# Value projection of two attention mixers: weight channels standing and tokens streaming, with transposes, instead of tokens standing

## The chip, the cores and the metric

The kernel runs on one core of a Trainium2 chip. Its time is the device time of one execution in microseconds (us). The engines named below are TensorE (PE, with its weight loads PEld), VectorE (DVE), ScalarE (ACT), GpSimd (POOL) and SyncE (SP), which here only issues DMA.

## The reference

One decoder layer over 2048 tokens of width 1024, in float32. An input projection feeds three mixers whose outputs are joined; then come an output projection, a layer norm, a gated feed-forward part with a short convolution, and a second layer norm.

```python
def _token_mixer(h, w_in, conv_w, a_log, dt_bias, gdn_norm_w, lam_vecs, diff_norm_w, w_out, lam_init):
    proj = h @ w_in
    a_qkv, a_z, a_b, a_dec, b_qkv, c_qkv = jnp.split(proj, np.cumsum(IN_SPLITS)[:-1], axis=-1)
    y_a = _gated_deltanet(a_qkv, a_z, a_b, a_dec, conv_w, a_log, dt_bias, gdn_norm_w)
    y_b = _dilated_window_group(b_qkv)
    y_c = _diff_attention_group(c_qkv, lam_vecs, diff_norm_w, lam_init)
    return jnp.concatenate([y_a, y_b, y_c], axis=-1) @ w_out
```

`b_qkv` (768 channels) belongs to the dilated window attention, `c_qkv` (768) to the differential attention. Of each, 256 channels are the values; these 512 value channels are what the change is about. The attention multiplies softmax weights by values, and for this the values are wanted with tokens in the rows (partitions).

## The kernel before, in words

*Blocks of tokens.* The tokens are worked in four blocks of 512 (`TB`). For each block t there is a job "A" (the projections of the two softmax mixers, `Projection.project`), a job "G" (those of the gated delta net), "d" and "w" (differential and dilated attention), and "f" (feed-forward). The lists `FIRST`, `SECOND` and `THIRD` (L1374 to L1376) give the order in which the jobs are written: A0 G0 A1 G1 d0 w0 first; then the steps of the delta net ("i" and "b" the inverse, "p" preparation, "r" recurrence) with G2, G3 and A3 among them; then w1 d1 A2 and the rest with the feed-forward part. A planner (the `TileContext`, L1451) orders the instructions of each engine by its own simulated times, so instructions of d0, which is written after G1, stand between those of A0. Each engine, and each queue of DMA issues, then works strictly in that order.

*Products in three parts.* Each product is made of float32 numbers split into a rounded high part and a low part, as three matmuls: high by high, high by low, low by high. `Dense.weights` (L127) brings a weight of 512 KB in two halves of 256 KB: it loads a raw half (L151), rounds it to the high part on ScalarE (L153) and subtracts on GpSimd for the low part (L154). Raw halves have six buffers, high and low halves four each in A0, A1 and A3. From the job "c0" on (`dn.keep`), the first use of a weight also writes both parts to DRAM (L161), and each later use loads them from there instead (`whi<-whi_d` and `wlo<-wlo_d`, L148), with no cast or subtraction. A0 and A1 come before c0, A3 is the first after it, and A2 comes later.

*Queries and keys.* `Dense.product` (L198) makes one 128 channel x 512 token product: the weight is the standing operand, the tokens stream, 8 x 3 matmuls of 128x512 into one PSUM bank. Before it starts it calls `flush(1)`, which counts down the steps that were put off with `put(n, step)` and writes out those that are due. `Projection.split` (L627) takes the result out of PSUM.

*Values.* `Projection.values` (L642) does it the other way: 128 tokens are the standing operand and 512 value channels stream, so that the result has tokens in its rows. It takes two groups of two token tiles; each group holds two PSUM banks for its whole length and goes through all eight k steps, so each of the four value weights (`w_val`, two k steps each) is brought twice per block, and each use serves 2 x 2 x 3 = 12 matmuls. Each bank is copied out on ScalarE (L662) into `vo`, and SP issues two writes (L663, L664): to `wv_d` (dilated) and `fv_d` (differential). `vo` shares the two buffers of the tag "y" with the results of the queries and keys.

*PSUM.* The tag "d" has two banks for A0 and A1, three for A3, four for A2.

Of the kernel before, what the change touches and what calls it, by code (L numbers as in the profile page):

```python
# [7 lines left out]
F32 = mybir.dt.float32  # L8
# [5 lines left out]
P = 128  # L14
T = 2048
D = 1024
KD = D // P
NB = 4
TB = T // NB
# [71 lines left out]
SLOT = 0.65  # L91
# [19 lines left out]
class Dense:  # L111
# [15 lines left out]
    def weights(self, src, k=KD, m=P, pool=None, key=None):  # L127
# [6 lines left out]
        def put(dt, name):  # L134
# [4 lines left out]
            else:  # L139
                w = self.wp.tile([P, TB], dt, tag=name, name=name, bufs=NRAW if name == "wraw" else NHALF)  # L140
            return shape(w[:, 0:n])

        his, los = [], []
        for i in range(2):
# [4 lines left out]
            else:  # L149
                raw = shape((self.wp.tile([P, TB], F32, tag="w" if self.ring else "wraw", name="wraw", bufs=self.ring or NRAW))[:, 0:n])  # L150
                nc.sync.dma_start(out=raw, in_=src[:, i * (k // 2) : (i + 1) * (k // 2)])  # L151
# [469 lines left out]
class Projection:  # L621
# [20 lines left out]
    def values(self, x, wide, near):  # L642


        nc, dn = self.nc, self.dn
        for g in range(2):
            ps = [dn.ps.tile([P, TB], F32, tag="d", name="vp") for _ in range(2)]
            for j in range(KD // 2):
                whi, wlo = dn.weights(self.I["w_val"][j], k=2, m=TB, key=("val", j))
                for a in range(2):  # L650
                    k = 2 * j + a
                    for i in range(2):
                        sl = slice((2 * g + i) * P, (2 * g + i + 1) * P)
                        xhi, xlo = (v[k][:, sl] for v in x)
                        nc.tensor.matmul(out=ps[i], lhsT=xhi, rhs=whi[:, a], start=(k == 0), stop=False)
                        nc.tensor.matmul(out=ps[i], lhsT=xhi, rhs=wlo[:, a], start=False, stop=False)
                        nc.tensor.matmul(out=ps[i], lhsT=xlo, rhs=whi[:, a], start=False, stop=(k == KD - 1))
                        yield SLOT
            for i in range(2):
                n = 2 * g + i  # L660
                vo = self.ap.tile([P, 2, 2, 2, P], F32, tag="y", name="vo", bufs=NY)[:, 0]
                nc.scalar.copy(vo, ps[i].rearrange("p (a b c) -> p a b c", a=2, b=2))  # L662
                nc.sync.dma_start(out=wide[n * P : (n + 1) * P], in_=vo[:, 0])  # L663
                nc.sync.dma_start(out=near[:, :, n], in_=vo[:, 1])  # L664

    def project(self, t, blocks, pool=None):
        nc, tc, I, dn, ap = self.nc, self.tc, self.I, self.dn, self.ap
# [370 lines left out]
class Ffn:  # L1038
# [131 lines left out]
    def turn(self, r, x):  # L1170
        nc, dn = self.nc, self.dn
        for k in range(KD):
            tp = dn.ps.tile([P, 4, P], F32, tag="d", name="tp")
            for tt in range(4):
                nc.tensor.transpose(tp[:, tt], r[tt][:, k * P : (k + 1) * P], self.ident)
            hi, lo = dn.split(tp.rearrange("p a b -> p (a b)"))
            x[0].append(hi)
            x[1].append(lo)
            yield 0.5
# [92 lines left out]
def decoder(tc, I, out, y_d=None, upto=3):  # L1272
    nc = tc.nc
    with ExitStack() as ctx:
# [52 lines left out]
        gates.close()  # L1327
        dn.wp, dn.ring = ctx.enter_context(tc.tile_pool(name="wp2", bufs=1)), NW
        psd2 = ctx.enter_context(tc.tile_pool(name="psd2", bufs=2, space=PSUM))
# [25 lines left out]
LAG_NT = 2  # L1355
NKS = 4
NW = 14
NRAW = 6
NHALF = 4
NXR = 4  # L1360
NPD = 6
NP = 4
NY = 2
# [15 lines left out]
def host_arrays(inputs):  # L1379
# [3 lines left out]
    a = {}  # L1383
    x = f("x")[0]
    a["xT"] = np.ascontiguousarray(x.reshape(NB, TB, KD, P).transpose(0, 2, 3, 1))

    def tiles(w):
        k, c = w.shape
        return np.ascontiguousarray(w.reshape(k // P, P, c // P, P).transpose(2, 1, 0, 3))
# [7 lines left out]
    a["gdn_a_log"] = np.ascontiguousarray(f("gdn_a_log"))  # L1397

    att = w_in[:, 2056:3592]
    a["w_att"] = tiles(np.concatenate([att[:, 0:512], att[:, 768:1280]], 1))  # L1400
    val = np.concatenate([att[:, 512:768], att[:, 1280:1536]], 1)
    a["w_val"] = np.ascontiguousarray(val.reshape(4, 2, P, TB).transpose(0, 2, 1, 3))
    a["diff_norm"] = np.ascontiguousarray(np.tile(f("diff_norm")[0], 2).reshape(P, 1))
    a["diff_lambda"] = np.ascontiguousarray(f("diff_lambda").reshape(1, 128))

# [15 lines left out]
    i = np.arange(P)  # L1421
    d = i[:, None] - i[None, :]
# [32 lines left out]
```

## Time and profile before

| what | us |
|---|---|
| median of 3 runs | 3210.19 |
| lowest and highest | 3209.55, 3212.74 |
| the profiled execution | 3217.71 |
| its span, first to last instruction | 3216.0 |

The profile describes one execution. Starts are in us from the start of the span; "busy" is the sum of durations with overlaps counted once; what stands in brackets behind an instruction is the idle time of its engine just before it and what released it. Matmuls are pipelined, so the distance between two starts is less than the duration shown. PEclk and "clock" are the granted clock of TensorE as a share of full speed. The mean clock over the execution is 0.964.

### The profile page before, as it was taken

How to read it: one execution, taken by the hardware profiler on the slowest of the kernel's cores; microseconds unless marked ns; L12 is line 12 of the kernel's file. 1: busy time of each engine (PE TensorE's matmuls, PEld its weight loads, DVE VectorE, ACT ScalarE, POOL GpSimd, SP SyncE). 2: the span in 40 equal slices, each digit the busy share in tenths (PEclk: the TensorE clock that was granted, in tenths of full speed). 3: DMA queues.
4: the chain of work that ended last, by engine and by line, in shares of the span. 5: the costliest groups of instructions: out<-in, count | busy, mean ns of one | idle time of the engine just before them, and what ended most of it. 6: DMA issues, size and time to landing. Idle time of an engine off the chain costs nothing.

```text
span 3216.0 us, 43559 instructions
## 1 busy us (share of the span) xinstructions
PE 2999.8 (93%) x14476; PEld 2310.5 (72%) x14476; DVE 1883.0 (59%) x3392; ACT 1358.5 (42%) x3188; POOL 751.0 (23%) x741
## 2 busy tenths in 40 slices
PE   7898989998688699999999999999999999999998
PEld 5676867777467577766777667777778764788887
DVE  2572659665436247855688445556777644474446
ACT  3653453644234134755565343223365545222213
POOL 4563555444332015555141000000000000000001
PEclk9998989999789799999999999999999999999999
DMA  7546464547788688777878446567486644666554
GB/s 212 168 140 203 136 202 140 154 148 217 271 247 299 197 275 272 261 244 238 272 250 266 155 157 205 175 212 246 150 264 202 190 150 125 203 233 195 191 187 147
DMA packets 463329, 659.30 MB, mean 205 GB/s; under 512 B 75168, under 2 KB 201632, under 8 KB 462336
## 3 DMA queue, kind: packets, MB, share of 16 engines
q1 hardware_dynamic: 425024, 567.36, 56.3%
q10 hardware_dynamic: 24480, 44.58, 3.8%
q0 software_dynamic: 13600, 44.58, 3.7%
q8 instruction: 115, 1.88, 0.2%
q14 instruction: 110, 0.90, 0.1%
HBM read 500.82 MB, written 155.39 MB: 204 GB/s over the span
## 4 chain that ended last, share of the span: by engine, by line
PE 62%; DMA 7%; DVE 5%; ACT 2%; issue 1%; SPq 1%; POOL 1%; ACTq 0%; DVEq 0%; POOLq 0%
PE d L206 10%; PE d L207 10%; PE d L208 10%; PE rp L1158 6%; PE rp L1159 6%; PE rp L1161 6%; PE bank L818 4%; PE bank L833 2%; PE bank L767 1%; PE bank L997 1%; DMA whi<-whi_d 1%; PE bank L1004 1%; PE bank L958 1%; DMA fq_d<-sy 1%; DVE nm L772 1%
## 5 line engine op out<-in xcount | busy, mean ns | idle before, releaser
L206 PE MATMUL d<-xhi,whi 128*128 128x512 f32 x2144 | 857.5, 400 | 47.4 <-DMA whi<-whi_d 16.1
L208 PE MATMUL d<-xhi,wlo 128*128 128x512 f32 x2144 | 854.0, 398 | 2.1 <-POOL wlo L154 2.1
L207 PE MATMUL d<-xlo,whi 128*128 128x512 f32 x2144 | 853.1, 398 | 1.3 <-DVE xlo L169 1.3
L154 POOL TENSOR_TENSOR wlo<-wraw,whi 128x512 fp32r<-128x512 f32 x370 | 504.8, 1369 | 1112.0 <-ACT whi L153 897.1
L206 PEld LDWEIGHTS d<-xhi,whi 128*128 128x128 f32 x2144 | 409.4, 191 | 153.3 <-DMA whi<-whi_d 17.2
L208 PEld LDWEIGHTS d<-xhi,wlo 128*128 128x128 f32 x2144 | 408.7, 191 | 105.4 <-issue 16.2
L207 PEld LDWEIGHTS d<-xlo,whi 128*128 128x128 f32 x2144 | 409.5, 191 | 100.2 <-issue 15.0
L153 ACT CAST whi<-wraw 128x512 fp32r<-128x512 f32 x370 | 227.9, 619 | 274.2 <-DMA wraw<-in_w_up 67.0
L1159 PE MATMUL rp<-wlo,hhi 128*128 128x512 f32 x704 | 278.2, 396 | 0.1
L1158 PE MATMUL rp<-whi,hhi 128*128 128x512 f32 x704 | 271.3, 399 | 0.7 <-DVE xlo L169 0.4
L843 POOL TENSOR_SCALAR_AFFINE_SELECT pd<-pd 128x128 f32<-128x128 f32 x64 | 27.4, 430 | 1013.2 <-DVE pd L839 993.5
L1161 PE MATMUL rp<-whi,hlo 128*128 128x512 f32 x672 | 263.9, 396 | 0.0
L776 ACT ACTIVATE bank<-bank,nm 128x512 f32<-128x512 f32 (+3 forms) x320 | 191.1, 598 | 107.4 <-DVE nm L772 66.2
L1090 ACT COPY ub<-d 128x512 f32<-128x512 f32 x172 | 100.8, 586 | 267.6 <-PE d L208 265.2
L839 DVE SCALAR_TENSOR_TENSOR pd<-pe,f_nlam,pd 128x512 f32<-128x512 f32 (+3 forms) x160 | 113.5, 715 | 168.1 <-ACT pe L835 142.6
L772 DVE TENSOR_REDUCE nm<-bank 128x1 f32<-128x512 f32 (+3 forms) x288 | 167.3, 596 | 73.2 <-PE bank L767 68.3
L1158 PEld LDWEIGHTS rp<-whi,hhi 128*128 128x128 f32 x704 | 132.4, 189 | 38.4 <-issue 7.1
L365 DVE SCALAR_TENSOR_TENSOR yc<-ub,i_taps,yc 128x512 f32<-128x512 f32 x144 | 156.5, 1087 | 3.3
L1159 PEld LDWEIGHTS rp<-wlo,hhi 128*128 128x128 f32 x704 | 132.9, 189 | 34.1 <-issue 6.3
L1161 PEld LDWEIGHTS rp<-whi,hlo 128*128 128x128 f32 x672 | 126.8, 189 | 30.8 <-issue 4.0
L1168 DVE TENSOR_TENSOR r<-r,rp 128x512 f32<-128x512 f32 x152 | 101.6, 683 | 79.8 <-PE rp L1161 74.0
L818 PE MATMUL bank<-pd,fv 128*64 128x512 f32 (+3 forms) x320 | 144.7, 554 | 1.4 <-POOL pd L843 0.6
(283 smaller groups left out, 4676.1 us busy)
## 6 DMA issues: line engine op xcount, KB each, us to landing
whi<-whi_d SPq DMA_DIRECT2D x486, 256.0 KB
wlo<-wlo_d SPq DMA_DIRECT2D x486, 256.0 KB
whi_d<-whi ACTq DMA_DIRECT2D x170, 256.0 KB
wlo_d<-wlo POOLq DMA_DIRECT2D x170, 256.0 KB, 3.7
wraw<-in_w_gdn SPq DMA_DIRECT2D x128, 256.0 KB
ks<-fk_d SPq DMA_DIRECT2D x160, 196.0 KB
wraw<-in_w_up SPq DMA_DIRECT2D x86, 256.0 KB
wraw<-in_w_down SPq DMA_DIRECT2D x50, 256.0 KB
```

The costliest lines, as they stand in the source:

```text
L153: nc.scalar.copy(hi, raw)
L154: nc.gpsimd.tensor_tensor(out=lo, in0=raw, in1=hi, op=ALU.subtract)
L206: nc.tensor.matmul(out=ps, lhsT=whi[:, k], rhs=xhi[k], start=(k == 0), stop=False)
L207: nc.tensor.matmul(out=ps, lhsT=whi[:, k], rhs=xlo[k], start=False, stop=False)
L208: nc.tensor.matmul(out=ps, lhsT=wlo[:, k], rhs=xhi[k], start=False, stop=(k == KD - 1))
L365: nc.vector.scalar_tensor_tensor(out=yc, in0=ub[:, j : j + TB], scalar=self.taps[:, mt, j : j + 1], in1=yc, op0=ALU.mult, op1=ALU.add)
L772: nc.vector.tensor_reduce(out=o, in_=s[:, 0:nf], axis=mybir.AxisListType.X, op=ALU.min)
L776: nc.scalar.activation(out=s[:, 0:n], in_=s[:, 0:n], func=AF.Exp, scale=-1.0, bias=o, accum_out=den[:, b, m, qt : qt + 1])
L818: nc.tensor.matmul(out=po[64 * hh : 64 * hh + 64, q0:], lhsT=v[:, 64 * hh : 64 * hh + 64], rhs=pd[hh][:, q0:], start=start, stop=stop)
L1158: nc.tensor.matmul(out=ps, lhsT=hi[:, sl], rhs=whi, start=first, stop=False)
L1159: nc.tensor.matmul(out=ps, lhsT=hi[:, sl], rhs=wlo, start=False, stop=last and lo is None)
L1161: nc.tensor.matmul(out=ps, lhsT=lo[:, sl], rhs=whi, start=False, stop=last)
```

## The change

Values are made like queries and keys: four products of 128 value channels by 512 tokens, with the weight standing. Their weights are appended to `w_att` (tiles 8 to 11), so each is brought once per block and serves 24 matmuls. Each product is copied out to `cm` (four buffers, shared with the raw tokens), and a put-off step turns it: four transposes of 128x128 into one bank of the tag "d", one copy to `vo`, one write issued by ScalarE. With `LAG_VALUES` = 1 the step of product c is written out before product c + 2 starts; `dn.flush()` at the end writes out what is left. Products 0 and 1 are the dilated values, 2 and 3 the differential ones.

```diff
-        for g in range(2):
-            ps = [dn.ps.tile([P, TB], F32, tag="d", name="vp") for _ in range(2)]
-            for j in range(KD // 2):
-                whi, wlo = dn.weights(self.I["w_val"][j], k=2, m=TB, key=("val", j))
-                for a in range(2):
-                    k = 2 * j + a
-                    for i in range(2):
-                        sl = slice((2 * g + i) * P, (2 * g + i + 1) * P)
-                        xhi, xlo = (v[k][:, sl] for v in x)
-                        nc.tensor.matmul(out=ps[i], lhsT=xhi, rhs=whi[:, a], start=(k == 0), stop=False)
-                        nc.tensor.matmul(out=ps[i], lhsT=xhi, rhs=wlo[:, a], start=False, stop=False)
-                        nc.tensor.matmul(out=ps[i], lhsT=xlo, rhs=whi[:, a], start=False, stop=(k == KD - 1))
-                        yield SLOT
-            for i in range(2):
-                n = 2 * g + i
-                vo = self.ap.tile([P, 2, 2, 2, P], F32, tag="y", name="vo", bufs=NY)[:, 0]
-                nc.scalar.copy(vo, ps[i].rearrange("p (a b c) -> p a b c", a=2, b=2))
-                nc.sync.dma_start(out=wide[n * P : (n + 1) * P], in_=vo[:, 0])
-                nc.sync.dma_start(out=near[:, :, n], in_=vo[:, 1])
+        for c in range(4):
+            pp = yield from self.product(8 + c, x)
+            cm = dn.xp.tile([P, TB], F32, tag="xraw", name="vc", bufs=NXR)
+            nc.scalar.copy(cm, pp)
+
+            def turn(c=c, cm=cm):
+                tp = dn.ps.tile([P, 4, P], F32, tag="d", name="vt")
+                for n in range(4):
+                    nc.tensor.transpose(tp[:, n], cm[:, n * P : (n + 1) * P], dn.ident)
+                vo = self.ap.tile([P, 2, 4, P], F32, tag="y", name="vo", bufs=NY)[:, 0]
+                nc.scalar.copy(vo, tp)
+                to = wide.rearrange("(n p) i c -> p n i c", p=P)[:, :, c] if c < 2 else near[:, c - 2]
+                nc.scalar.dma_start(out=to, in_=vo)
+
+            dn.put(LAG_VALUES, turn)
+        dn.flush()
...
+LAG_VALUES = 1
...
-    a["w_att"] = tiles(np.concatenate([att[:, 0:512], att[:, 768:1280]], 1))
-    val = np.concatenate([att[:, 512:768], att[:, 1280:1536]], 1)
-    a["w_val"] = np.ascontiguousarray(val.reshape(4, 2, P, TB).transpose(0, 2, 1, 3))
+    a["w_att"] = tiles(np.concatenate([att[:, 0:512], att[:, 768:1280], att[:, 512:768], att[:, 1280:1536]], 1))
```

## Rows read from the trace of the kernel before

**Rows 1.** The page's first two parts: busy time of each engine, and the span in 40 slices of 80 us, in tenths, for TensorE and its granted clock.

```profile
PE 2999.8 (93%) x14476; PEld 2310.5 (72%) x14476; DVE 1883.0 (59%) x3392; ACT 1358.5 (42%) x3188; POOL 751.0 (23%) x741
...
PE   7898989998688699999999999999999999999998
...
PEclk9998989999789799999999999999999999999999
```

**Rows 2.** Busy time by stretch: the stretch and its length, then PE, PEld, DVE, ACT and POOL busy with the number of instructions, then granted clock, DMA share and GB/s. A0, A1, the first and second half of A3, A2.

```profile
63.60:111.20 47.60, 33.70 (x131) 26.22 (x129) 18.89 (x86) 28.48 (x82) 19.08 (x15) 0.86 0.63 202
289.00:329.50 40.50, 35.03 (x174) 26.58 (x174) 11.52 (x32) 18.18 (x37) 19.87 (x16) 0.92 0.63 216
855.80:895.60 39.80, 20.57 (x49) 11.37 (x47) 8.01 (x21) 3.58 (x6) 10.89 (x12) 0.58 0.79 279
905.00:934.50 29.50, 27.23 (x238) 22.55 (x237) 7.62 (x20) 8.44 (x23) 5.30 (x6) 0.86 0.88 256
1141.70:1188.20 46.50, 40.67 (x230) 31.31 (x229) 17.60 (x50) 12.44 (x23) 2.15 (x2) 0.93 0.82 276
```

**Rows 3.** The instructions that write or read the tile `vo`: duration in ns (least, median, most), first and last start.

```profile
L662 ACT COPY vo<-vp x16: 559/587/602, 92.3 to 1188.7; 128x512 f32<-128x512 f32 x16
L663 SPq DMA_DIRECT2D wv_d<-vo x16: 319/382/1099, 93.6 to 1189.5; - x16
L664 SPq DMA_DIRECT2D fv_d<-vo x16: 525/562/1403, 94.7 to 1190.1; - x16
```

**Rows 4.** TensorE in order of time around A0's values: start, duration, instruction, and in brackets the idle time before it and its releaser.

```profile
77.26 0.66 PE L767 MATMUL bank<-ks,qs 96*128 96x384 f32 x1 [4.05 <-DMA ks<-fk_d]
...
91.95 1.52 PE L767 MATMUL bank<-ks,qs 96*128 96x128 f32 x4 [6.39 <-ACT whi L153]
...
97.30 0.63 PE L657 MATMUL vp<-whi,xlo 128*128 128x512 f32 x1
97.73 0.63 PE L655 MATMUL vp<-whi,xhi 128*128 128x512 f32 x1
...
112.09 0.50 PE L334 MATMUL d<-xhi,i_wba 128*128 128x512 f32 x1 [0.87 <-ACT vo L662]
```

**Rows 5.** SP's queue of DMA issues in order of time in the same stretch.

```profile
69.08 0.53 SPq L151 DMA_DIRECT2D wraw<-in_w_val  x1
76.00 0.31 SPq L741 DMA_DIRECT2D qs<-fq_d  x1
...
78.50 2.36 SPq L151 DMA_DIRECT2D wraw<-in_w_val  x2
89.02 0.34 SPq L736 DMA_DIRECT2D ks<-fk_d  x1
89.45 0.33 SPq L151 DMA_DIRECT2D wraw<-in_w_val  x1
...
90.73 1.78 SPq L151 DMA_DIRECT2D wraw<-in_w_val  x4
```

**Rows 6.** A1's values, in order of time: two instructions of TensorE, and one line of SP's queue.

```profile
303.76 0.43 PE L997 MATMUL bank<-pts,vw 128*64 128x128 f32 x2 [1.75 <-ACT pts L1007]
...
313.37 0.79 PE L655 MATMUL vp<-whi,xhi 128*128 128x512 f32 x1 [3.72 <-ACT vo L662]
...
299.44 14.46 SPq L151 DMA_DIRECT2D wraw<-in_w_val  x7
```

**Rows 7.** TensorE's waits over the whole span, grouped by who waited for whom: us in total, times, the longest.

```profile
PE vp L655 <- ACT whi L153: 17.7, 5, 5.5
...
PE vp L655 <- DMA whi<-whi_d: 7.1, 2, 5.6
```

**Rows 8.** ScalarE's waits from 855 to 897 us, in the same form.

```profile
ACT whi L153 <- DMA x_d<-fs: 8.3, 1, 8.3
...
ACT whi L153 <- DMA r<-in_x: 6.4, 1, 6.4
ACT whi L153 <- DMA wraw<-in_w_val: 5.4, 1, 5.4
```

**Rows 9.** From the page's groups of instructions (busy us, mean ns of one, idle time before) and of DMA issues (count, KB each): the subtraction, the cast, the loads from the DRAM copies and the raw loads of value weights.

```profile
L154 POOL TENSOR_TENSOR wlo<-wraw,whi 128x512 fp32r<-128x512 f32 x370 | 504.8, 1369 | 1112.0 <-ACT whi L153 897.1
...
L153 ACT CAST whi<-wraw 128x512 fp32r<-128x512 f32 x370 | 227.9, 619 | 274.2 <-DMA wraw<-in_w_up 67.0
...
whi<-whi_d SPq DMA_DIRECT2D x486, 256.0 KB
...
wraw<-in_w_val SPq DMA_DIRECT2D x40, 256.0 KB
```

**Rows 10.** Transposes of the dilated attention (L1004): their group; then, in order of time, a set of four of them between value matmuls of A1; then the busy times of the stretch from 296 to 301 us, in which 14 of them stand (columns as in rows 2).

```profile
L1004 PE MATMUL bank<-d_ident,p 128*128 128x128 f32 x400 | 67.0, 279 | 1.2 <-DVE p L978 1.2
...
297.82 0.60 PE L1004 MATMUL bank<-d_ident,p 128*128 128x128 f32 x4
298.18 0.48 PE L656 MATMUL vp<-wlo,xhi 128*128 128x512 f32 x1
298.49 0.39 PE L657 MATMUL vp<-whi,xlo 128*128 128x512 f32 x1
298.72 0.39 PE L656 MATMUL vp<-wlo,xhi 128*128 128x512 f32 x1
...
296.00:301.00 5.00, 5.00 (x30) 4.21 (x29) 1.18 (x2) 0.59 (x2) 2.88 (x3) 1.00 0.26 91
```

## Prediction

> **What bounds the kernel now.** I read the page's first two parts first. TensorE is busy 93% of the span, and in the slices it is at 9 from about 1,250 us on; what it loses it loses before, in the same slices in which the granted clock drops [rows 1]. So the end is set by TensorE's stream, and a change counts by what it adds to that stream and by the waits it takes out of the first 1,200 us. DMA, VectorE and ScalarE count only where TensorE waits for them.
>
> Next I cut out the four stretches in which the value matmuls run, with the busy time of each engine [rows 2]. They belong to A0 (63.6 to 111.2 us), A1 (289.0 to 329.5), A3 (855.8 to 934.5, in two halves with 9 us of other work between) and A2 (1141.7 to 1188.2). The same 96 matmuls are worth 96 x 0.23 = 22 us in each: 0.23 us lies between two starts where nothing is late, though the duration shown is 0.39 (298.49 to 298.72) [rows 10]. TensorE is idle for 47.6 - 33.7 = 13.9 us in A0's stretch, 5.5 in A1's, 39.8 - 20.6 = 19.2 and 2.3 in A3's halves, 5.8 in A2's. The mean clocks are 0.86, 0.92, 0.58, 0.86 and 0.93: after a wait a dozen matmuls start 0.43 apart instead of 0.23 (97.30, 97.73) [rows 4], the lower of the clock's two levels, 1.2 instead of 2.4 GHz.
>
> Last, the instructions themselves, to see what each wait is for.
>
> - A0: 6.39 us at 91.95, for the cast of a value weight; 4.05 at 77.26 is for keys of d0 [rows 4]. SP's queue shows why: nothing is issued from 69.6 to 76.0 and from 80.9 to 89.0 us, and then what stands first is a load of d0's queries or keys; the value weights are behind it [rows 5].
> - A1: 1.75 us, and 3.72 until the two PSUM banks of the first half are copied out; seven value loads take 14.46 us to be issued [rows 6].
> - A3: of the waits before value matmuls, five (17.7 us) are for the cast of a value weight, one per half load, which does only 6 matmuls [rows 7]. In that stretch ScalarE waits 5 to 8 us at a time for DMA before a cast [rows 8].
> - A3's second half and A2: 7.1 us in two waits, the longer 5.6 (A2's), for weights read back from their DRAM copies [rows 7].
>
> **The change, part by part.** *Matmuls*: 96 per block before, 4 x 8 x 3 = 96 after, of the same shape. Nothing.
>
> *Weights.* A value weight of 512 KB is used for 12 matmuls before and for 24 after, so there are 4 fetches per block and not 8. The raw loads go from 40 [rows 9] to 24 (A0 and A1 eight fewer each; A3 had read its second half back), and the loads from the copies fall by 16 + 16 (A3: 8 + 8, A2: 8 + 8). That is 48 x 256 KB = 12.6 MB. In A0 and A1 also 16 casts of 0.62 us on ScalarE and 16 subtractions of 1.37 on GpSimd go [rows 9]; neither engine was the bound there. What the waits are worth then:
>
> - A0: seven of the sixteen value loads are issued after 69.6 us [rows 5], so nine were out before the gaps, and eight is now all there is. At most 6.39 and the low clock after (13 matmuls x 0.2 = 2.6) go: 9.0. The keys of d0 and G0's weights are late next, on the same queue, so I take 8; at the least 0.
> - A1: with seven loads from 299.44 on [rows 6], nine of the sixteen were issued before; eight are needed. 1.75 + 3.72 + 2.6 for the low clock = 8.1 can go. The dilated block that shares the stretch is late next; I take 7, at the least 0.
> - A3: eight raw half loads remain with all their stores, so the pace of the loads from 855.8 to 895 stays, but each now carries 12 matmuls. The 17.7 us of waits and 30 x 0.2 = 6 us of low clock have room for the other 48 matmuls (11 us), and 4.2 MB of read-back go from the stretch behind. At most 17.7 + 6 = 23.7 is gained. But behind it stand the inverse and the recurrence, steps that wait for one another: in the second half TensorE has 238 matmuls in 29.5 us, of which 48 are ours [rows 2]. I take 9; at the least 0.
> - A2: 16 read-backs fewer of 32; 5.6 + 2.6 = 8.2 can go. I take 6; at the least 0.
>
> Sum 8 + 7 + 9 + 6 = 30 us; ends 0 and 49.0.
>
> *Transposes.* 4 per product, 16 products, 64 in all, on TensorE's stream. The nearest rows are those of the dilated block, same shape and same identity: four of them hold up the next matmul by 0.36 us (297.82 to 298.18) and its successor by 0.08 more [rows 10]. 16 x 0.44 = 7.0 us. With their mean duration of 0.279 us laid end to end they would be 17.9; the rows show them overlapped, so I take 7.0 and keep 17.9 for the bound.
> The Trainium skill speaks against this part: "TensorE: Matmul & The Clock Gate", section "Part 4: PE-mode transpose", puts a transpose at about 275 ns in a kernel and says that it does not count as work for the clock. By that duration the sum would be 64 x 0.275 - 7.0 = 10.6 us worse. The spacing of the rows does not agree with it, and the stretch from 296 to 301 us, with 14 transposes between matmuls, has a clock of 1.00 [rows 10]. So I keep 7.0 and make the clock a rival.
>
> *Copies and waits.* Eight copies out of PSUM per block, not four: 16 more of 0.587 us [rows 3], 9.4 us of ScalarE, which is idle for over a third of each stretch; hidden. The transposes of product c are put behind the matmuls of product c + 1, 24 x 0.23 = 5.5 us later, so the copy they need is done unless ScalarE is stuck. Where it is not hidden: with two banks (A0, A1) the products and the transposes share them, so products 2 and 3 want a bank whose copy has only begun; and the last transposes of each block follow their copy directly. The row for such a wait is 0.87 us (G0's first matmul, which waited for the copy of a value block) [rows 4]. That makes 2 + 2 + 4 = 8 places, but before had two such places in A0 and A1 each; 4 x 0.87 = 3.5 us. Ends: 0, if other matmuls are put there, and 8 x 0.87 = 7.0.
>
> *Queues.* The value writes leave SP (32 issues of 0.38 and 0.56 us [rows 3], 15 us in all) and become 16 issues of twice the size on ScalarE. At 0.56 that is 9 us over the run, 18 if an issue grows with its size. Behind each stand casts and exponentials, which have slack for a microsecond: nothing. SP gains issue time where it mostly stood still: nothing. The near values now come last (products 2 and 3), so d0's second part can ask for its first values up to 8 us later than it did; G0's matmuls cover that, and without that cover it is 8 us once, in A0.
>
> Sum: -30 + 7.0 + 3.5 = -19.5 us. The profiled run took 3217.71 us (span 3216.0 and 1.7 around it), 7.5 above the median of the runs; the difference is taken off the median: 3210.19 - 19.5 = 3190.7.
>
> **The rivals.**
>
> *All waits go.* Every cap is reached, the copies are hidden: -49.0 + 7.0 = -42.0, 3168.2 us. For it: each of these waits has a value weight or its read-back as its cause. Against it: SP's gaps in A0 and the chain behind A3 are not the values' own.
>
> *The waits move on.* A0, A1 and A3 wait as long for the keys, the window tiles and the inverse, and only A2 (6) and A1's bank wait (3.7) go: -9.7 + 10.5 = +0.8, 3211. For it: 4.05 us in A0 are already a wait for keys, and DMA is 0.79 to 0.88 busy in A3's halves [rows 2]. Against it: the bytes fall just where DMA is fullest.
>
> *Copies stuck behind casts (the slower side).* ScalarE works in order. In A3 a cast waits 5 to 8 us for its load [rows 8]. If the copy that frees a product's bank, or that its transposes need, stands behind such a cast, TensorE stops with it. Were that so for all four products of A3 at 6.5 us, and A3 gained nothing, the sum is -21 + 10.5 + 26 = +15.5, 3226 us. It decides from two stuck copies on: a loss of 13 against the 10.5 that are left without A3. Against it: the weights of a product are cast a product ahead, so the copy mostly stands in front.
>
> *The clock.* As a mechanism of this kernel: each of 16 sets of transposes is followed by 14 matmuls at 0.43 us, 16 x 2.8 = 45 us, so 3190.7 + 45 = 3236. Rows 10 speak against it. It is what the skill's sentence on the clock would come to.
>
> **How the numbers follow.** The forecast, a gain of 10 to 32 us: 0.46. All waits go: 0.20. They move on: 0.18. Stuck copies: 0.13. The clock: 0.03. The planner makes the order of all instructions anew, which is the main reason for a wide range: 3163 (5 us under the fullest gain) to 3216 (moved-on waits with 5 us more for copies and transposes); that leaves out most of the two slower cases and the rim of the fullest. The forecast's own range is 3178 to 3200. About 0.2%, 6.4 us, is what can be told from no change. Faster takes the first two cases and a little of the third, 0.68; within 0.2% most of the third, 0.16; slower the rest, 0.16.
>
> **What would show it.** In the profile after, value weights count among the attention weights: 24 raw loads more of these, and 470 loads from each kind of copy instead of 486 [rows 9]. In A3's stretch the waits for a cast are fewer or carry 12 matmuls each, and no value weight is read back. The transposes start some 0.1 us apart and hold up matmuls by under 0.5 us per set. It is wrong if TensorE's idle time before 1,200 us is as long as now, or if waits of several us stand before transposes or before a product's first matmul, released by a copy.

## The result, and the profile after

| | before | after |
|---|---|---|
| median (us) | 3212.74 of 7 runs | 3195.15 of 7 runs |
| lowest and highest | 3209.55, 3219.54 | 3191.23, 3204.87 |
| profiled execution, its span | 3217.71, 3216.0 | 3204.87, 3203.2 |

The ratio after to before is 0.9949, 95% interval 0.9935 to 0.9962: 16.4 us faster (17.6 between the medians), where 19.5 were forecast. The profiled execution of after is the slowest of its seven, 9.7 us above their median, so its trace shows a smaller gain (12.8 us) than the medians.

The page's first part, and the groups that answer to [rows 9]:

```profile
PE 2992.4 (93%) x14540; PEld 2318.5 (72%) x14540; DVE 1887.7 (59%) x3392; ACT 1348.6 (42%) x3186; POOL 726.1 (23%) x725
...
L154 POOL TENSOR_TENSOR wlo<-wraw,whi 128x512 fp32r<-128x512 f32 x354 | 479.6, 1359 | 1140.2 <-ACT whi L153 920.3
...
whi<-whi_d SPq DMA_DIRECT2D x470, 256.0 KB
wraw<-in_w_att SPq DMA_DIRECT2D x72, 256.0 KB
```

The fetches are the ones counted ahead: 16 subtractions fewer (370 to 354), 16 read-backs fewer of each kind, 24 raw value loads among the 72 in place of 40. Line numbers past L645 differ from before; L649 copies a product to `vc`, L654 are the transposes, L656 the copy to `vo`, L658 the writes.

Busy time by stretch, columns as in [rows 2], for the stretches in which the value products of A0, A1, A3 and A2 now run:

```profile
70.00:104.00 34.00, 28.07 (x115) 21.80 (x115) 10.14 (x51) 15.74 (x47) 8.94 (x8) 0.85 0.58 188
283.00:314.00 31.00, 27.43 (x140) 22.08 (x141) 9.39 (x27) 11.85 (x26) 7.70 (x6) 0.94 0.59 196
847.00:902.00 55.00, 31.01 (x154) 23.98 (x152) 13.39 (x32) 10.81 (x19) 19.37 (x23) 0.78 0.85 285
1136.00:1184.50 48.50, 41.87 (x256) 33.17 (x251) 16.09 (x52) 15.23 (x29) 11.01 (x12) 0.93 0.82 277
```

TensorE is idle for 5.9, 3.6, 24.0 and 6.6 us in them, where it was 13.9, 5.5, 19.2 + 2.3 and 5.8. So A0 improved most, A1 a little, and A3 and A2 did not, as far as idle time tells it: the stretches are shorter than before and hold other amounts of other work.

*A0.* SP's queue, as in [rows 5]: the last value load (the raw `in_w_att` at 66.30) is now issued before the gap from 71.2 to 77.6 us, and what stands behind the gaps are weights of G0.

```profile
66.30 3.01 SPq L151 DMA_DIRECT2D wraw<-in_w_att  x1
...
70.67 0.53 SPq L151 DMA_DIRECT2D wraw<-in_w_gdn  x1
77.60 0.31 SPq L738 DMA_DIRECT2D qs<-fq_d  x1
```

TensorE's waits there, as in [rows 4]: the 6.39 us for a cast are gone, and what is late next is the exponential of a differential attention bank (3.50 us). The first matmul of G0 starts at 103.65, not 112.09 [rows 4].

```profile
79.04 0.30 PE L764 MATMUL bank<-ks,qs 96*128 96x128 f32 x1 [0.93 <-DMA ks<-fk_d]
...
89.39 2.51 PE L764 MATMUL bank<-ks,qs 96*128 96x384 f32 x5 [3.50 <-ACT bank L773]
...
103.29 0.60 PE L654 MATMUL vt<-d_ident,vc 128*128 128x128 f32 x4
103.65 0.48 PE L334 MATMUL d<-xhi,i_wba 128*128 128x512 f32 x1
```

The last two lines also price a set of four transposes: the next matmul starts 0.36 us later.

Both waits came to TensorE through ScalarE. The matmul that waited 6.39 us is one of d0, and d0's exponentials stood on ScalarE behind a cast that had waited 6.52 us for its value weight (first line, before). In after, ScalarE issues its first value write only after 8.3 us of standing still, put down to a write of d0's keys that had not landed, and the exponentials behind it are the ones for which TensorE waits 3.50 us (the other two lines):

```profile
89.65 0.62 ACT L153 CAST whi<-wraw 128x512 fp32r<-128x512 f32 x1 [6.52 <-DMA wraw<-in_w_val]
```

```profile
88.44 0.39 ACTq L658 DMA_DIRECT2D wv_d<-vo  x1
88.88 0.34 ACT L773 ACTIVATE bank<-bank,nm 128x128 f32<-128x128 f32 x1 [8.72 <-DMA fk_d<-sy]
```

*A3.* The waits for a cast ([rows 7], 17.7 us) have become one wait for a cast (6.8) and three before transposes (13.7 in all). TensorE, in order of time:

```profile
864.09 0.79 PE L206 MATMUL d<-xhi,whi 128*128 128x512 f32 x1 [6.76 <-ACT whi L153]
...
873.34 1.12 PE L654 MATMUL vt<-d_ident,vc 128*128 128x128 f32 x4 [8.03 <-ACT vc L649]
...
886.07 0.66 PE L654 MATMUL vt<-d_ident,vc 128*128 128x128 f32 x4 [2.38 <-ACT vc L649]
886.49 0.47 PE L206 MATMUL d<-xhi,whi 128*128 128x512 f32 x1
886.80 0.39 PE L207 MATMUL d<-xlo,whi 128*128 128x512 f32 x1
...
900.80 1.11 PE L654 MATMUL vt<-d_ident,vc 128*128 128x128 f32 x4 [3.33 <-ACT vc L649]
```

And ScalarE, which had the copy at 872.70 to make, behind a write to the copies (872.33) and 8.66 us of waiting for a DMA:

```profile
863.43 0.61 ACT L153 CAST whi<-wraw 128x512 fp32r<-128x512 f32 x1
872.33 0.33 ACTq L161 DMA_DIRECT2D whi_d<-whi  x1
872.70 0.58 ACT L649 COPY vc<-d 128x512 f32<-128x512 f32 x1 [8.66 <-DMA r<-in_x]
```

*A2.* The 5.6 us for a read-back are gone, and at about the same place a wait of 6.63 us stands before transposes of the dilated attention, for exponentials that VectorE then scales; ScalarE had them behind a cast that waited 15.22 us for a feed-forward weight (TensorE's line, then ScalarE's two, each from its own timeline):

```profile
1164.31 1.11 PE L1001 MATMUL bank<-d_ident,p 128*128 128x128 f32 x4 [6.63 <-DVE p L975]
```

```profile
1161.85 0.62 ACT L153 CAST whi<-wraw 128x512 fp32r<-128x512 f32 x1 [15.22 <-DMA wraw<-in_w_up]
1162.38 0.93 ACT L973 ACTIVATE p<-p,dnm 128x768 f32<-128x768 f32 x1
```

### The profile page after: what moved, and what is told of

Same layout as the page of the kernel before. It is cut to its first block, busy times and chain, and to the rows that moved or that the text cites. A ratio compares the mean times of both kernels' runs of the same rounds, so it can differ in the third digit from the quotient of the medians.

```text
span 3203.2 us, 43526 instructions
## 1 busy us (share of the span) xinstructions
PE 2992.4 (93%) x14540; PEld 2318.5 (72%) x14540; DVE 1887.7 (59%) x3392; ACT 1348.6 (42%) x3186; POOL 726.1 (23%) x725
## 4 chain that ended last, share of the span: by engine, by line
PE 69%; DMA 10%; DVE 9%; ACT 4%; issue 3%; SPq 1%; POOL 1%; ACTq 0%; POOLq 0%; DVEq 0%
PE d L206 12%; PE d L208 11%; PE d L207 11%; PE rp L1155 6%; PE rp L1156 6%; PE rp L1158 6%; PE bank L815 4%; PE bank L830 2%; DVE yc L365 2%; PE bank L994 2%; PE bank L1001 1%; DMA wraw<-in_w_att 1%; PE bank L764 1%; DMA fk_d<-sy 1%; DMA wraw<-in_w_up 1%
## 5 line engine op out<-in xcount | busy, mean ns | idle before, releaser
L206 PE MATMUL d<-xhi,whi 128*128 128x512 f32 x2272 | 914.9, 403 | 35.9 <-ACT whi L153 14.4
L208 PE MATMUL d<-xhi,wlo 128*128 128x512 f32 x2272 | 906.9, 399 | 16.8 <-DMA wlo<-wlo_d 14.3
L207 PE MATMUL d<-xlo,whi 128*128 128x512 f32 x2272 | 906.2, 399 | 0.8 <-DVE xlo L169 0.7
L154 POOL TENSOR_TENSOR wlo<-wraw,whi 128x512 fp32r<-128x512 f32 x354 | 479.6, 1359 | 1140.2 <-ACT whi L153 920.3
L206 PEld LDWEIGHTS d<-xhi,whi 128*128 128x128 f32 x2272 | 436.2, 192 | 152.0 <-issue 20.8
L208 PEld LDWEIGHTS d<-xhi,wlo 128*128 128x128 f32 x2272 | 435.9, 192 | 124.6 <-DMA wlo<-wlo_d 16.2
L207 PEld LDWEIGHTS d<-xlo,whi 128*128 128x128 f32 x2272 | 436.3, 192 | 99.6 <-issue 9.3
L153 ACT CAST whi<-wraw 128x512 fp32r<-128x512 f32 x354 | 217.8, 618 | 291.8 <-DMA wraw<-in_w_up 97.0
L769 DVE TENSOR_REDUCE nm<-bank 128x1 f32<-128x512 f32 (+3 forms) x288 | 166.9, 595 | 72.8 <-PE bank L764 64.8
L1087 ACT COPY ub<-d 128x512 f32<-128x512 f32 x172 | 100.7, 585 | 256.3 <-PE d L208 254.4
L1158 PEld LDWEIGHTS rp<-whi,hlo 128*128 128x128 f32 x672 | 126.4, 188 | 30.5 <-issue 3.8
L1092 DVE SCALAR_TENSOR_TENSOR yg<-ub,c_taps,yg 128x512 f32<-128x512 f32 x176 | 143.1, 813 | 3.7
```

Source lines behind the costliest of these rows:

```text
L153: nc.scalar.copy(hi, raw)
L154: nc.gpsimd.tensor_tensor(out=lo, in0=raw, in1=hi, op=ALU.subtract)
L206: nc.tensor.matmul(out=ps, lhsT=whi[:, k], rhs=xhi[k], start=(k == 0), stop=False)
L207: nc.tensor.matmul(out=ps, lhsT=whi[:, k], rhs=xlo[k], start=False, stop=False)
L208: nc.tensor.matmul(out=ps, lhsT=wlo[:, k], rhs=xhi[k], start=False, stop=(k == KD - 1))
L769: nc.vector.tensor_reduce(out=o, in_=s[:, 0:nf], axis=mybir.AxisListType.X, op=ALU.min)
```

## The experiments

The theory at the start was the prediction's: the time is won where value weights are fetched half as often. Against it stood that the change gives the planner another program, and that the order it makes carries the net. The table shows where TensorE loses time in each kernel's profiled execution. "Lost" is worked out from the trace: the time that passed, less a usual spacing for every matmul that started in it (the 30th percentile, over all fourteen traces, of the distance from a matmul of that line and operation to the next start). Spacings taken by line and shape as well shift whole columns, by up to 15 us, but the differences between kernels by some 2 us at most; so differences are what the table tells. The ratio is that of the runs to before.

| kernel | ratio | lost 0 to 400 us | 400 to 850 | 850 to 1000 | 850 to 1100 | 1150 to 1250 | behind 1250 |
|---|---|---|---|---|---|---|---|
| before | 1 | 79.3 | 97.6 | 62.0 | 97.2 | 21.8 | 138.8 |
| after | 0.9949 | 63.8 | 106.2 | 52.8 | 99.5 | 20.5 | 128.3 |
| e1: new in A0, A1 | 0.9960 | 58.4 | 108.4 | 51.4 | 99.8 | 14.0 | 125.0 |
| e2: new in A3, A2 | 0.9965 | 78.4 | 94.7 | 49.4 | 99.0 | 19.9 | 130.3 |
| e3: fetched twice | 1.0062 | 83.6 | 101.0 | 56.6 | 93.8 | 21.8 | 139.0 |
| e4: no transposes | 0.9983 | 59.1 | 118.3 | 54.5 | 97.3 | 19.7 | 126.4 |
| e5: copy on VectorE | 0.9942 | 59.3 | 106.1 | 49.8 | 103.9 | 16.8 | 124.3 |
| e6: lag 2 | 0.9959 | 66.1 | 100.9 | 48.8 | 103.2 | 19.7 | 126.9 |
| e7: before, writes on ScalarE | 1.0028 | 81.2 | 91.5 | 66.0 | 100.7 | 24.8 | 139.6 |
| e9: loads of A0, A1 twice | 0.9991 | 76.3 | 94.3 | 50.9 | 98.9 | 20.9 | 130.9 |
| e10: new in A2 | 1.0008 | 78.2 | 94.4 | 57.6 | 101.5 | 14.9 | 136.1 |
| e11: new in A3 | 1.0039 | 78.2 | 94.3 | 46.7 | 99.6 | 21.4 | 144.5 |
| e12: e5 without A2 | 1.0015 | 60.4 | 105.1 | 49.7 | 104.0 | 23.4 | 141.6 |
| e13: e11, A2 reads copies | 1.0092 | 79.4 | 93.0 | 48.6 | 99.7 | 37.3 | 147.0 |

**The new way in A0 and A1 only, and in A3 and A2 only.**

```diff
-        yield from self.values(x, wv_d, v_d)
+        yield from (self.values if t < 2 else self.values_before)(x, wv_d, v_d)
```

The second has `t >= 2`; `values_before` is the old function.

> The new way of making values in A0 and A1 alone; A3 and A2 keep the old one. Theory F (the gain comes from fewer fetches of value weights, in the stretches that were starved of them): G1's first matmul comes 15 to 19 us earlier than in the kernel before, as it does in the changed kernel (18.7), and most of it lasts: 8 to 16 us off the whole time, ratio 0.995 to 0.9975. Theory P (the planner's new order of everything moves the time by as much as the change does, and the parts do not add up): the lead is there at G1 but the end lies within 5 us of before on either side.

> The new way in A3 and A2 alone. Theory F: 3 to 10 us off the whole time, ratio 0.997 to 0.999, and together with the run on A0 and A1 the two come to the 17.6 us of the whole change within 6 us. Theory P: the sum of the two misses 17.6 us by more than 8. Theory R (what A3 gains is lost to the recurrence behind it): the stretch to the last of A3's values is 15 to 30 us shorter, but the last transpose of the recurrence comes within 3 us of where it was, and the end too.

Measured: 0.9960 [0.9945, 0.9975] and 0.9965 [0.9954, 0.9977], 12.8 and 11.2 us; together 24, where the whole change gives 16.4. (The traced execution of the first took 3185.23 us, 15 under the median of its runs, 3200.01.) Around the first matmul of G1 (L334), in order of time, first with the new way in A0 and A1; then that matmul alone, in the second kernel, in before and in after:

```profile
307.64 0.60 PE L677 MATMUL vt<-d_ident,vc 128*128 128x128 f32 x4
307.99 0.48 PE L334 MATMUL d<-xhi,i_wba 128*128 128x512 f32 x1
```

```profile
331.20 0.48 PE L334 MATMUL d<-xhi,i_wba 128*128 128x512 f32 x1
```

```profile
332.12 0.48 PE L334 MATMUL d<-xhi,i_wba 128*128 128x512 f32 x1
```

```profile
313.39 0.48 PE L334 MATMUL d<-xhi,i_wba 128*128 128x512 f32 x1
```

24.1 us of lead against 0.9. So the lead at 330 us belongs to A0 and A1 (after itself has 18.7 us). In the second kernel A3's last value instruction on TensorE starts 32.3 us earlier than before (901.3 for 933.6) and the recurrence's last matmul 9.2 us earlier (1056.94 for 1066.17), so theory R does not hold as it was put.

**The loads alone, given back.** In A0 and A1 each raw value weight is loaded a second time into a buffer of the same tag, and not cast, subtracted or used.

```diff
+            w = dn.weights(self.I["w_att"][8 + c], key=("att", 8 + c))
+            for i in range(2 if t < 2 else 0):
+                more = dn.wp.tile([P, TB], F32, tag="wraw", name="wmore", bufs=NRAW)
+                nc.sync.dma_start(out=more, in_=self.I["w_att"][8 + c][:, 4 * i : 4 * i + 4])
-            pp = yield from self.product(8 + c, x)
+            pp = yield from self.product(8 + c, x, w)
```

> The changed kernel with each raw value weight of A0 and A1 loaded a second time into the raw buffers, and neither cast nor subtracted: the loads of before (16 per block) with the casts and subtractions of after (8). If A0 and A1 were starved by the loads and SP's queue, as the prediction has it, their gain of 15 to 20 us goes: G1's first matmul within 6 us of before and ratio 0.998 to 1.002. If ScalarE's casts and GpSimd's subtractions were what starved them, G1 keeps a lead of 12 us or more and the ratio stays at 0.994 to 0.997.

Measured: 0.9991 [0.9981, 1.0000]; of 16.4 us gained, 13.5 are lost again (0.9991 - 0.9949 of 3212). G1's first matmul stands at 326.59: of the lead of 18.7, 5.5 are left. TensorE's waits from 280 to 330 us show what is late: window keys of the dilated attention, which share SP's queue with the second loads.

```profile
PE bank L959 <- DMA kw<-wk_d: 10.7, 1, 10.7
PE bank L959 <- DVE dnm L966: 3.1, 1, 3.1
```

So the lead at 330 us is made by the loads on SP's queue with the raw buffers that they hold, and little of it by the casts and subtractions. The kernel can't tell issues from buffers, nor from the bytes moved. The 13.5 us at the end are another matter: by 850 us this kernel has lost 170.6 us and after 170.0, so the lead that the loads took away made no difference any more by then, and where the end time was lost is not shown.

**Each value weight fetched twice in all four blocks.**

```diff
-            pp = yield from self.product(8 + c, x)
+            w = [dn.weights(self.I["w_att"][8 + c], key=("att", 8 + c)) for _ in range(2)]
+            w = tuple(Halves([w[0][i].parts[0], w[1][i].parts[1]]) for i in range(2))
+            pp = yield from self.product(8 + c, x, w)
```

> The changed kernel, but every value weight is fetched twice, and half of each copy is used, so that loads, casts and subtractions are as many as before (A3's second fetch reads the DRAM copy); transposes and writes stay new. Theory F: the gain goes and the added work stays, 8 to 12 us slower than before: 3220 to 3225 us, ratio 1.0025 to 1.004. Theory P: the fetches do not matter by themselves, and the time stays within 8 us of the changed kernel, 3187 to 3203.

Measured: 3230.16 us, 1.0062 [1.0050, 1.0074], slower than before by 19.9 us, more than the 8 to 12 expected. G1's first matmul stands at 336.40, so no lead is left. In A3 the second fetch reads back what was just written; TensorE's longest wait there, in order of time:

```profile
903.05 0.80 PE L206 MATMUL d<-xhi,whi 128*128 128x512 f32 x1 [27.32 <-DMA whi<-whi_d]
```

The new way without its smaller number of fetches is thus a loss; the 27.3 us of this one wait are a price that neither kernel pays, so the 35 us to after overstate what the fetches are worth.

**No transposes.** `vo` is copied from `cm` as it stands.

```diff
-                tp = dn.ps.tile([P, 4, P], F32, tag="d", name="vt")
-                for n in range(4):
-                    nc.tensor.transpose(tp[:, n], cm[:, n * P : (n + 1) * P], dn.ident)
...
-                nc.scalar.copy(vo, tp)
+                nc.scalar.copy(vo, cm.rearrange("p (n q) -> p n q", n=4))
```

> The changed kernel without the 64 transposes and their PSUM banks (values are copied from the untransposed tile instead; the copies and writes stay, so the values reach the attention with channels in the rows). Priced as predicted: 7.0 us for the transposes and up to 3.5 for waits, so 3185 to 3188 us. If the copies stuck behind casts in A3 cost their full 13.7 us: 3174 to 3180. If the waits only move to the next thing that is late: within 4 us of the changed kernel.

Measured: 3204.76 us, 0.9983 [0.9974, 0.9993]: 64 transposes less, and some 11 us slower than with them. None of the three expectations came. The traces don't show where the 11 us lie, since the two traced executions took about the same (3203.33 and 3204.87 us); what stands out in them is a loss between 400 and 850 us (118.3 against 106.2), far from any value product. So the transposes' price can't be read from the end of a kernel. That the planner's new order takes more than they cost is the likeliest cause, not a shown one. What the transposes are worth stands in the sum of usual spacings, 2758.0 us with them and 2751.9 without: 6.1 us (6.9 to 7.0 by other workings of the spacing).

**The product's copy on VectorE; the put-off steps one product later.**

```diff
-            nc.scalar.copy(cm, pp)
+            nc.vector.tensor_copy(cm, pp)
```

and, in a kernel of its own, `LAG_VALUES = 2`.

> The changed kernel with the product's copy out of PSUM on VectorE instead of ScalarE. Theory S (copies stuck behind casts cost real time): the 13.7 us of waits before transposes in A3 fall under 3, and the time drops 5 to 13 us below the changed kernel's, ratio to before 0.991 to 0.9935. Theory O (the planner's new order moves the time by some 10 us whatever is edited, as the run without transposes did, which did less work and took 11 us more than the changed kernel): those waits go and the time still lies anywhere within 10 us of the changed kernel.

> The changed kernel with the transposes put off by one product more (LAG_VALUES 2); the same instructions, only written later. Theory S: the waits before transposes in A3 fall by half, 3 to 7 us faster than the changed kernel, ratio 0.993 to 0.994. Theory O: within 10 us on either side, with no tie to those waits; the first 400 us stay as in the changed kernel (lost time of TensorE 60 to 65 us by then, 79 before).

Measured: 0.9942 [0.9929, 0.9954] and 0.9959 [0.9946, 0.9971]. Both are what after is, within the intervals; the first is the fastest kernel measured, by too little to be told from it. The wait that each was to remove became smaller, 8.9 and 7.3 us for 13.7, but the first was to bring it under 3, and in the second, where it was to halve and did, a wait for a cast grew to 15.8 us from 6.8 (third group, 840 to 905 us):

```profile
PE vt L654 <- DVE vc L649: 8.9, 4, 6.8
```

```profile
PE vt L654 <- ACT vc L649: 7.3, 2, 3.8
```

```profile
PE d L206 <- ACT whi L153: 15.8, 1, 15.8
```

In A3 the waits for copies and casts thus sum to 16.3 and 23.1 us, where after has 20.5. Neither brought anything by 1100 us (103.9 and 103.2 lost from 850 on, against 99.5).

**Before, with its value writes issued by ScalarE.**

```diff
-                nc.sync.dma_start(out=wide[n * P : (n + 1) * P], in_=vo[:, 0])
-                nc.sync.dma_start(out=near[:, :, n], in_=vo[:, 1])
+                nc.scalar.dma_start(out=wide[n * P : (n + 1) * P], in_=vo[:, 0])
+                nc.scalar.dma_start(out=near[:, :, n], in_=vo[:, 1])
```

> The kernel before with one part of the change alone: the 32 value writes are issued by ScalarE. Theory F (the fetches are what matters): no gain in the stretches of A0 and A1, G1's first matmul within 4 us of before, and the whole time within 0.2% of before but for what the new order does. Theory O: the whole time differs from before by 5 to 12 us on either side, with the difference behind 400 us.

Measured: 1.0028 [1.0016, 1.0040]. Taking the writes off SP's queue wins nothing by itself (81.2 lost in the first 400 us, and G1's first matmul at 335.08, 3.0 us later than before), so the gain in A0 and A1 is not theirs.

**One block at a time.** With `t == 2`, with `t == 3`, and with `t != 2` together with the copy on VectorE:

> The new way in A2 alone. As predicted (6 us less wait, 2 to 3 us of transposes and copies): 0 to 6 us faster, ratio 0.998 to 1.000. Against it, theory W (the wait only changes its name): the changed kernel lost 85 us of TensorE from 1000 to 1250 us where the kernel before lost 77, so A2 alone is 0 to 8 us slower, 1.000 to 1.0025, but for what the order does elsewhere.

> The new way in A3 alone. As predicted: 9 us less wait against 2 to 3 of added work, 6 to 7 us faster, ratio 0.9975 to 0.9985. If the recurrence behind A3 takes it all back: 0.9995 to 1.0015, with the last of A3's values 15 us or more earlier and the last transpose of the recurrence within 3 us. Together A0 and A1 alone (0.9960), A3 alone and A2 alone should come to 0.9949 if the parts add up.

> The new way in A0, A1 and A3 with the product's copy on VectorE, the old way in A2: what the runs so far would make the best version. If A2 is where the change loses: 0.990 to 0.993, faster than the changed kernel by 6 to 14 us. If the order decides: within 10 us of the changed kernel on either side.

Measured: 1.0008 [0.9997, 1.0018], 1.0039 [1.0025, 1.0054], 1.0015 [1.0003, 1.0027]. These mixes carry a price of their own that the expectations overlooked: A3 writes the copies that A2 reads, and where the two blocks use different layouts A2 finds none, loads and casts anew and writes copies again, in all three. From the page of the kernel with A3 alone, and from TensorE's waits there:

```profile
whi_d<-whi ACTq DMA_DIRECT2D x178, 256.0 KB
```

```profile
PE vp L654 <- ACT whi L153: 8.7, 3, 4.0
```

170 such writes are in before and after. The first agrees with theory W, the other two with neither of theirs. So the ratios do not say what one block is worth; the stretches up to 1100 us, ahead of A2, still do.

**A3 alone, with A2's old way reading A3's copies.**

```diff
+            if key is not None and key[0] == "val" and self.vals:
+                hi, lo = put(F32R, "whi"), put(F32R, "wlo")
+                at = (2 * key[1] + i) * P
+                for part, d in zip((hi, lo), self.vals):
+                    nc.sync.dma_start(out=cast(part[:, 0].rearrange("p (c m) -> p c m", c=4)), in_=cast(d[:, :, at : at + P]))
-            if key in self.kept:
+            elif key in self.kept:
```

> The new way in A3 alone, as in e11_a3_only, but A2's old way now reads its value weights from the copies that A3's new way wrote (the four tiles of each part stand side by side in one DRAM tile; a half is read as 128 x 4 pieces of 512 B, in one DMA as before). In e11_a3_only A2 found no copies of its own kind: it loaded and cast its eight raw halves and wrote them out (178 writes to the copies in place of 170), and TensorE waited 8.7 us there for casts that are not in the kernel before nor in the kernel after. Theory X, that those casts made A3 alone slow: the wait for casts before A2's matmuls is gone, and the ratio is 0.995 to 1.000, some 10 us under e11_a3_only and near e2_last_two (0.9965). Theory Y, that A3's own lead is given back behind it and the new order costs the rest: the writes are 170 again, but the ratio stays at 1.002 to 1.005. Under both, TensorE has lost less than before by 1000 us (some 10 us less from 850 on) and waits before A3's transposes for a copy.

Measured: 1.0092 [1.0073, 1.0110], slower still, and under neither theory: the casts are gone, but the function still wrote out, once, what it had just read back, so the writes are again 178. They stand on ScalarE in front of other work. Two of ScalarE's waits from 1140 to 1260 us, put down to read-backs, each of an instruction right behind such a write:

```profile
ACT p L1007 <- DMA whi<-whi_d: 12.3, 1, 12.3
...
ACT pts L1038 <- DMA wlo<-wlo_d: 8.6, 1, 8.6
```

TensorE then waits 7.95 us for the exponentials and 3.48 for the other copy; from 1150 to 1250 us it loses 37.3 instead of 21.8. The run settles nothing on A3's share of the end time. Up to 1100 us it is a second kernel with A3 alone in the new way, and there it says what the others say. To see what that is, the stretch from 1000 to 1100 us (columns as in [rows 2]) and then TensorE's longest waits in it, first of before and then of after:

```profile
1000.00:1100.00 100.00, 77.10 (x384) 63.99 (x382) 49.43 (x106) 31.05 (x77) 4.77 (x5) 0.86 0.75 234
```

```profile
PE yp L598 <- POOL on L595: 8.5, 3, 6.9
PE pv L564 <- DVE R L560: 6.4, 1, 6.4
PE po L579 <- DVE S L572: 1.7, 1, 1.7
```

```profile
1000.00:1100.00 100.00, 68.39 (x340) 56.84 (x338) 43.60 (x98) 27.84 (x68) 4.59 (x5) 0.84 0.54 167
```

```profile
PE yp L598 <- POOL on L595: 13.9, 2, 7.0
PE po L579 <- DVE S L572: 6.2, 4, 3.6
PE pv L564 <- DVE R L560: 5.2, 3, 3.5
PE pS L569 <- ACT vn L566: 2.1, 3, 0.8
```

These are steps of the recurrence, in which TensorE waits for VectorE and GpSimd. All such waits (`pk`, `pv`, `pS`, `po`, `yp`) sum to 20.6 us before and 27.4 after. In the ten kernels with the new A3 the sum is 25.7 to 28.8 (21.2 in the one that fetched twice and had waited 27 us just before), in the four with the old A3 20.3 to 22.6. So 6 to 7 us more are waited in the recurrence where A3 is new. That this is A3's gain, waited away, fits the sums but isn't shown: the recurrence's last matmul (`yp`) starts at 1066.17 us in before, 1063.66 in after and 1051.69 with A3 alone, but at 1056.63 with A2 alone, a kernel whose A0, A1 and A3 are those of before. So the planner's order, or chance between executions, moves this place by 9.5 us without A3, as much as A3's gain.

## Why the prediction was right or wrong

The time was right within 5 us: 3195.15 against 3190.7, inside the likeliest case's own range. The working behind it was right for the transposes and, up to the next job's first matmul, for A0 and A1; it was wrong for A3, for A2 and for the queues.

- *A0 8, A1 7 us.* Right in place and cause, and too small for that place: 8.4 us of lead at G0's first matmul (112.09 to 103.65) and 10.3 more by G1's, 18.7 in all, where 15 less 3.5 for 32 transposes were taken. e1, e2, e3 and e9 show that the fetches make it, and e9 that it is the loads, as SP's queue had suggested. What was not foreseen is how much is given back: the five kernels with fewer fetches in A0, A1 and with transposes have lost 17.5 us less than the six with the old way there by 400 us (means 61.6 and 79.1), but only 6.5 less by 850 (166.9 and 173.4). Where it goes between was not tried out.
- *A3 9 us.* This is the step that failed. By 1000 us the new way had lost 8.5 us less (means 50.8 and 59.3), about as taken; by 1100 us nothing is left (99.9 over ten kernels, 99.8 over four). But the 8.5 are a mean of two cases: with A0 and A1 as before it is 13.7 (48.2 in three kernels, 61.9 in three), with A0 and A1 new only 1.1 (50.3 in after, e5, e6 and e12, 51.4 in e1, the one kernel with the old A3 there). In the changed kernel itself, then, A3 gained next to nothing even by 1000 us. The prediction named the cover, "the inverse and the recurrence, steps that wait for one another", and still left 9 us of 23.7 on the account. The rival of the stuck copies also came in part: 13.7 us before transposes in A3 behind ScalarE's waits, with 6.8 for a cast, in place of the 17.7 for casts.
- *A2 6 us.* Wrong: from 1150 to 1250 us, 19.9 lost on average with the new way in A3 and A2 (seven kernels, 16.8 to 21.8), 20.2 with the old way in both (three, 14.0 to 24.8). The read-back's wait went and a wait of 6.63 us for exponentials took its place, as in the rival "the waits move on".
- *Transposes 7.0 us.* Right: 6.1 to 7.0 by usual spacings. A set at 103.29 holds up the next matmul by 0.36 us and the one after by some 0.08, as in [rows 10]. The rival of the clock falls: the Trainium skill ("TensorE: Matmul & The Clock Gate", "Part 4: PE-mode transpose") says that transposes do not count as work for the clock, but the mean clock is 0.966 against 0.964 before, and in the 8 us behind the wait at 886.07, with two sets of four, it is 1.00:

```profile
886.00:894.00 8.00, 6.62 (x32) 5.22 (x32) 0.00 (x0) 2.82 (x6) 4.08 (x5) 1.00 1.05 353
```

  Its figure for one in a kernel, about 275 ns, agrees with the duration here, 272 ns in the median, but as a price it is too high, since the four overlap.
- *Copies and waits 3.5 us.* Too small in one place: in A0 the waits behind a copy are 0.38 and 0.41 us, in A3 13.7 in three waits. The places were counted as if ScalarE were free; in A3 it waits for DMA in front of the copy. The prediction read [rows 8] as casts that wait for their loads. In order of time a write to the copies (L161) stands in front of each of those three casts, and ScalarE's wait ends with that write, here in before:

```profile
861.43 0.33 ACTq L161 DMA_DIRECT2D whi_d<-whi  x1
861.87 0.62 ACT L153 CAST whi<-wraw 128x512 fp32r<-128x512 f32 x1 [6.44 <-DMA r<-in_x]
```

  Over the run ScalarE stands still (for more than 0.5 us at a time) for 50.3 us right in front of 15 such writes in before, and for 42.7 in front of 12 in after. No kernel here takes them off ScalarE, so what they cost is open.
- *Queues, nothing.* This failed as well. In before the writes on ScalarE cost 0.28%, and a copy to `vo` waited 10.8 us for one of them. In the changed kernel ScalarE stands still for 17.4 us in front of three of its 16 value writes (issued at 88.44, 896.62 and 908.99 us), and TensorE waits 3.50 us at 89.39 and 1.96 at 909.99 for what stands right behind the first and the last. The issues themselves are cheaper than taken, 0.377 and 0.332 us in the median for 256 KB.

The prediction named two signs of being wrong: TensorE's idle time before 1,200 us as long as now, and waits of several us before transposes, released by a copy. Both came. The second is the wait of 8.03 us in A3. For the first, that stretch, first in before and then in after (columns as in [rows 2]):

```profile
0.00:1200.00 1200.00, 1021.16 (x5706) 822.59 (x5707) 637.50 (x1201) 517.66 (x1228) 470.70 (x426) 0.91 0.64 201
```

```profile
0.00:1200.00 1200.00, 1022.84 (x5782) 831.79 (x5783) 646.11 (x1211) 515.63 (x1236) 455.13 (x418) 0.92 0.61 193
```

Idle are 178.8 and 177.2 us. 76 more instructions are done in after, nearly all of them its transposes.

So what made the sum right? In the two profiled executions the loss falls by some 18 us and the work grows by 5.2, which leaves the 12.8 between them. Up to 1250 us the loss falls by 7.6; the other 10.5 come behind it (138.8 to 128.3), in the feed-forward stretch, where no instruction of the change stands. Six of the seven kernels with the new way in both A3 and A2 lie at 124 to 131 there and the mixed ones at 136 to 147, but of the three with the old way in both, one has 125.0 too (e1, whose traced execution was 15 us under its median). Single executions of one kernel differ by several us as well. Whether that term is the planner's order, the state in which A2 leaves the queues, or chance in two executions is open. As far as these two executions tell it, the sum came out by luck: A3's 9 and A2's 6 us did not come, and about as much came from a stretch that the prediction had at nothing.

## What to carry to other kernels

Fetching a weight half as often takes away waits where the trace shows the loads themselves late on an in-order queue, as in A0 and A1. Before crediting a saved wait to the end time, look at what stands behind it: of 18.7 us of lead at 330 us some 7 were left by 850, and A3's 8.5 us were gone 100 us later. A write moved to a computing engine's queue can hold that engine up: look at what its issue waits for, and at what stands behind it. Where a planner makes the order, even a kernel with less work was 11 us slower; judge parts by milestones in the trace, find out how far these move between kernels that are alike up to there, and check that a part left old does not lose what the other part used to prepare for it.

## What the runs showed of the hardware that was not expected

- A write that ScalarE issues waits in ScalarE's own order, and holds up what stands behind it: in after, exponentials right behind a value write had ScalarE idle for 8.72 us, put down to a DMA of SP's queue that had to land; in the last experiment, exponentials and a copy right behind writes of tiles that were being read back waited 12.3 and 8.6 us.
- Where A3 read a tile back from DRAM right after writing it, TensorE had one wait of 27.3 us (a DMA share of 0.84 from 850 to 905 us). How much of it is the write's wait on ScalarE, the queue or the load was not taken apart.
- One write of 256 KB from ScalarE's queue takes 0.33 to 0.38 us to issue; SP needed 0.38 + 0.56 us for the two halves of that size before [rows 3], and ScalarE 0.33 + 0.52 for the same two halves in before with the writes on ScalarE.
